# Another order of the seven products in the gate and up projections of a hybrid encoder block

## The chip, the cores and the metric

The kernel runs on one core of a Trainium2 chip. The metric is the device time of one execution in microseconds (us). TensorE multiplies; VectorE (DVE), ScalarE (ACT) and GpSimd (POOL) work on tiles, each taking the instructions of its own queue in order; SyncE (SP), ScalarE and GpSimd issue DMA transfers. GpSimd cannot reach the matmul banks (PSUM), so only VectorE and ScalarE read them.

## What is computed

One encoder block on x of 1024 rows by 1024 features, in float32:

```python
h = rmsnorm(x, norm1_g)
q, k, v, f_logit, u = split(h @ w_in)
attn = forgetting_attention(q, k, v, cumsum(log_sigmoid(f_logit + b_f)))   # 8 heads of 64
pool = multiscale_pool(u, w_pool, pool_scale)                              # windows 2, 4, 8, 16
x = x + concat(attn, pool) @ w_out
h2 = rmsnorm(x, norm2_g)
x = x + (silu(h2 @ w_gate) * (h2 @ w_up)) @ w_down                         # 1024 -> 2816 -> 1024
y = rmsnorm(x, final_g)
```

The change lies in the last product but one: `h2 @ w_gate` and `h2 @ w_up`, and the SwiGLU features made from them. The attention, the pooling, the first projections and the last norm are as they were.

## The kernel before

**Precision.** Every large product is done with operands split in two: ScalarE copies the source to a high part of reduced precision, VectorE subtracts it from the source for the low part (`split`, L119 to L121), and TensorE adds three matmuls, high x high, low x high and high x low (`mm3`, L159 to L163). A split weight operand of 128 x 1024 is called a page. Pages live in three slots that are used in turn (`gu_page`, L999), so the fourth page waits until TensorE is through with the first.

**Groups and products.** The 2816 features are worked in eleven groups (j = 0 to 10) of 256. In a group, the weights form a 2 x 2 block matrix (two halves of the features by two halves of the 1024 inputs), the normed rows another, and the four blocks of the result come from seven products P1 to P7 instead of eight (Strassen's scheme in Winograd's form). Four operands of the weight side are sums or differences, made by GpSimd in `gu_sums` (L1080): s1 = a21 + a22 for P5, s2 = s1 - a11 for P6, s3 = a11 - a21 for P7, s4 = a12 - s2 for P3; P1, P2 and P4 take a11, a12 and a22 as loaded. The raw halves (a11 and a12 in one buffer, a21 and a22 in the other) are loaded on SyncE's queue when the pages of the group before have been made (`gu_raw`, called in `next_page`, L1384 to L1388).

Each product is done for gate (n = 0) and up (n = 1), twelve matmuls of 512 columns each, into a pair of banks. P1, P6 and P5 add up in the same pair, c1, and after each of them ScalarE copies the pair out (`snap`, L1147, L1150): sP1 after P1, sU2 after P6, sU4 after P5. The next product of c1 must wait for the copy. P7 starts the pair c3 and P4 adds to it. `corner` (L1161) makes a feature block from c3 and a copy: h22 after P5 (c3 holds P7, with sU4), h21 after P3b (c3 holds P7 + P4, with sU2): VectorE adds the copy to gate (L1169) and up (L1171), ScalarE applies silu (L1170), GpSimd multiplies (L1172). h11 is sP1 + P2 and h12 is sU4 + P3. GpSimd then makes the sums f1 to f4 (L1176), and all blocks are stored by DMAs on ScalarE's queue (`spill`, L1272).

**Products in quarters.** In groups 1 to 10 P3, and in groups 3 to 10 (`BOTH = 3`) P2 as well, is split once more into seven quarter products Q1 to Q7 (`fine_product`, L1252), six matmuls of 256 columns each. VectorE adds each to the copy it belongs to (L1270). Three small banks hold them: Q1, Q6, Q5 and Q3 add up in bank A, Q7 and Q4 in bank B, Q2 is alone in C, and each of them has to wait until the add before it has read its bank. Their operands come in two pages, "a" (Q1, Q2, Q7, Q4) after one sum on VectorE and "b" (Q5, Q3, Q6) after three more (`fine_sums`, L1226 to L1231). The moving side needs small sums too, made once for P3 (b22) and once for P2 (b21) by the twelve `fine_steps` (L1187), spread over the product steps of groups 1 and 2.

**What sets the order.** A scheduler places the instructions of each engine by their readiness in its own timing model, with program order as priority; `tc.issue_after(ins)` puts what is traced in its block behind `ins` on the queue of the same engine. The main loop (L1393) goes through `todo`, with the products of groups 3 to 10 in the order `LAST`: P1, P6, P2a, P7, P2b, P5, P3a, P4, P3b. At each step it makes the page of the step after next, issues due stores, runs the product, and makes copies and features (`after`, L1279). `PIECES` (L1371) interleaves the quarters with a whole product: P2's with P7, P3's with P4. `mark` holds the last instruction of a kind: "page" and "hi" (last low and high part), "sum", "add" (last quarter add), "snap", "mm".

**Behind the groups** comes the output product with w_down, done in the same scheme over four sets of groups; its first pages and sums (`down_page`, L1358, `down_sum`, L1338) are made within group 10.

Of the kernel before, what the change touches and what calls it, by code (L numbers as in the profile page):

```python
# [45 lines left out]
def tile_kernel(  # L46
# [70 lines left out]
    mark = {}  # L117
# [956 lines left out]
    RING = 11  # L1074
# [5 lines left out]
    def gu_sums(j):  # L1080
        a11, a12, a21, a22 = gu_parts(j)
        s1, s2, s3, s4 = (xw_tile(f"s{i}", f"s{i}_{j}", (P, 2, 512)) for i in (1, 2, 3, 4))
        at = None
        for out, in0, in1, op in (
            (s1, a21, a22, ALU.add), (s2, s1, a11, ALU.subtract), (s3, a11, a21, ALU.subtract), (s4, a12, s2, ALU.subtract)
        ):
            with tc.issue_after(at.ins) if at and j >= BOTH else ExitStack():
                at = nc.gpsimd.tensor_tensor(out=out, in0=in0, in1=in1, op=op)  # L1088
        return dict(P1=a11, P2=a12, P6=s2, P7=s3, P5=s1, P3=s4, P4=a22)
# [57 lines left out]
    def snap(j, key, n):  # L1147
        tag = ("su", 2) if key == "sU2" else ("h", RING)
        t = snaps[j, key, n] = wk_tile(*tag, f"sn{j}_{key}{n}")
        mark["snap"] = nc.scalar.activation(out=t, in_=banks["c1", n], func=AF.Copy)  # L1150
# [101 lines left out]
    def fine_product(j, k, q, acc):  # L1252

        at = FINE_BANK[q]
        if q in ("Q1", "Q7", "Q2"):
            own = BANKS["c2", int(k == "P3")], 1
            fine_banks[at] = bank(f"fine{at}_{j}{k}", *(own if at == "C" else ("m", 2)))
        ps = fine_banks[at][:, QTR[0]]
        wh, wl = fine[j, k, q]
        bh, bl = fine[BLOCK[k], q]  # L1260
        for c in range(2):
            ws = slice(c * P, (c + 1) * P)
            mm3(
                ps, wh[:, ws], wl[:, ws], bh[:, c, :], bl[:, c, :],
                q in ("Q1", "Q7", "Q2") and c == 0, q in ("Q3", "Q4", "Q2") and c == 1, True,
            )
        n, h = FINE_TO[q]
        out = acc[n][:, QTR[h]]
        with tc.issue_after(mark["add"].ins) if q != "Q1" else ExitStack():
            mark["add"] = nc.vector.tensor_tensor(out=out, in0=ps, in1=out, op=ALU.add)  # L1270
# [97 lines left out]
    LAST = ("P1", "P6", "P2a", "P7", "P2b", "P5", "P3a", "P4", "P3b")  # L1368
# [5 lines left out]
    WINDOWS2 = {"P2a": (0, "P2", "P7"), "P7": (1, "P2", "P7"), "P2b": (2, "P2", "P7")}  # L1374
# [16 lines left out]

    waiting = []
    for i, (j, k) in enumerate(todo):  # L1393
        if i + 2 < len(todo) and k != "P2b":
            with ExitStack() as order:
                if k in ("P6", "P5") and j >= BOTH:
                    for ins in (mark["page"], mark["hi"]):
                        order.enter_context(tc.issue_after(ins.ins))
                    if k == "P5":
                        mark["P3a"] = mark["page"], mark["hi"]  # L1400
                        fine_sums(j, "P3", "b")
                        order.enter_context(tc.issue_after(mark["sum"].ins))
                next_page(*todo[i + 2])
        waiting.append(spills[:])
# [9 lines left out]
        elif k in window[j]:  # L1414
            step, little, whole = window[j][k]
            acc = [snaps[j, dict(P2="sP1", P3="sU4")[little], n] for n in range(2)]
            for piece in PIECES[step]:
# [8 lines left out]
        if k == "P2b":  # L1426
            with tc.issue_after(mark["add"].ins):
                next_page(*todo[i + 2])
        if (j, k) == (NG - 1, "P3b"):
            last_features = lambda j=j, k=k: after(j, k)  # L1430
        else:
            after(j, k)
        if j == NG - 1:
# [3 lines left out]
            if k == "P2a":  # L1437
                for key in ("P5", "P6"):
                    down_sum(0, key)
            if k == "P7":  # L1440
                for par in range(2):
                    down_load(par)
            if k == "P3a":
                with tc.issue_after(mark["add"].ins):
# [5 lines left out]
        if (j, k) == (BOTH - 1, "P1"):  # L1450
            q5, q7 = ([small(wk, f"g{n + m}", f"fine{n}{m}_b21") for m in range(2)] for n in (2, 4))
            finer += fine_steps("b21", q5, q7, ("g0", "g1"))
        for _ in range(min(3 if j == 1 and k in ("P1", "P2") else 2, len(finer))):
# [9 lines left out]
    with tc.issue_after(mark["add"].ins):  # L1463
        down_page(1)
# [178 lines left out]
```

## Time and profile before

| | |
|---|---|
| median of 3 runs | 1155.68 us (1153.98 to 1156.32) |
| profiled execution, its own time | 1151.23 us |
| its span, first to last instruction | 1149.4 us |
| mean granted clock of TensorE | 0.961 |
| TensorE busy, matmuls | 1054.1 us, 92% |
| VectorE busy | 797.8 us, 69% |
| ScalarE busy | 470.7 us, 41% |
| GpSimd busy | 412.8 us, 36% |

A profile is one execution, and times in it count from its first instruction. A row of the timeline has the start, the duration, the engine, the line of the kernel, the operation, the tile written and the tiles read, and in brackets how long the engine sat idle before it and what ended that. A row of the waits has the engine, tile and line that waited, what it waited for, and total, times and longest. Tile names leave numbers out: `gu_P` is a bank of the seven products, `gu_P_h` and `gu_P_l` the parts of a page, `r` the raw halves, `s` GpSimd's sums, `sn_sP` and `sn_sU` the copies, `b11`, `t2`, `t3`, `t1`, `t4` the moving blocks of P1, P6, P7, P5 and P4, `d` the output product.

### The profile page before, as it was taken

How to read it: one execution, taken by the hardware profiler on the slowest of the kernel's cores; microseconds unless marked ns; L12 is line 12 of the kernel's file. 1: busy time of each engine (PE TensorE's matmuls, PEld its weight loads, DVE VectorE, ACT ScalarE, POOL GpSimd, SP SyncE). 2: the span in 40 equal slices, each digit the busy share in tenths (PEclk: the TensorE clock that was granted, in tenths of full speed). 3: DMA queues.
4: the chain of work that ended last, by engine and by line, in shares of the span. 5: the costliest groups of instructions: out<-in, count | busy, mean ns of one | idle time of the engine just before them, and what ended most of it. 6: DMA issues, size and time to landing. Idle time of an engine off the chain costs nothing.

```text
span 1149.4 us, 15183 instructions
## 1 busy us (share of the span) xinstructions
PE 1054.1 (92%) x5428; PEld 895.5 (78%) x5428; DVE 797.8 (69%) x1224; ACT 470.7 (41%) x759; POOL 412.8 (36%) x316
## 2 busy tenths in 40 slices
PE   9999999999999979997977869797876899999997
PEld 8888889989888858886766757676765788888886
DVE  7365667668765958787566474655557589978787
ACT  7343556656643744342222232222223234333345
POOL 4430222133431507455355271726436340000035
PEclk9999999999999989999989889898989899999999
DMA  6225343237312513240321213131222576444423
GB/s 226 65 60 147 79 105 96 76 97 265 131 62 94 166 37 120 73 128 10 120 101 47 92 55 100 38 119 56 91 92 86 181 247 225 150 147 156 150 98 147
DMA packets 108859, 130.28 MB, mean 113 GB/s; under 512 B 8040, under 2 KB 71024, under 8 KB 108784
## 3 DMA queue, kind: packets, MB, share of 16 engines
q1 hardware_dynamic: 97216, 108.18, 30.0%
q10 hardware_dynamic: 10928, 19.42, 4.5%
q0 software_dynamic: 640, 1.71, 0.4%
q8 instruction: 43, 0.70, 0.2%
q14 instruction: 32, 0.26, 0.1%
HBM read 86.29 MB, written 33.03 MB: 104 GB/s over the span
## 4 chain that ended last, share of the span: by engine, by line
PE 33%; DVE 9%; POOL 4%; ACT 3%; DMA 3%; issue 2%; SPq 1%; POOLq 0%; ACTq 0%; DVEq 0%
PE d L162 5%; PE d L163 5%; PE d L161 5%; PE gu_P L161 5%; PE gu_P L162 4%; PE gu_P L163 4%; POOL s L1088 3%; DVE gu_P_l L121 2%; DMA r<-in_w_up_dram 2%; DVE s L1231 1%; ACT gu_P_h L120 1%; DVE gu_P3a_l L121 1%; DVE r L1231 1%; DVE sn_sU L1303 1%; SPq L1048 1%
## 5 line engine op out<-in xcount | busy, mean ns | idle before, releaser
L162 PE MATMUL d<-d,d 128*128 128x512 f32 (+1 forms) x308 | 119.2, 389 | 0.5 <-DVE d L121 0.5
L163 PE MATMUL d<-d,d 128*128 128x512 f32 (+1 forms) x308 | 119.0, 388 | 0.0
L629 POOL TENSOR_SCALAR p<-p,rr 128x128 f32<-128x128 f32 (+3 forms) x64 | 48.7, 768 | 176.0 <-DVE rr L628 131.8
L161 PE MATMUL d<-d,d 128*128 128x512 f32 x308 | 107.8, 388 | 0.0
L121 DVE TENSOR_TENSOR gu_P_l<-s,gu_P_h 128x1024 fp32r<-128x1024 f32 (+1 forms) x38 | 62.1, 1644 | 41.2 <-ACT gu_P_h L120 41.2
L161 PE MATMUL gu_P<-t2h,gu_P_h 128*128 128x512 f32 x88 | 43.2, 491 | 50.3 <-ACT sn_sP L1150 50.3
L120 ACT ACTIVATE d<-r_f 128x1536 fp32r<-128x1536 f32 (+1 forms) x28 | 38.7, 1384 | 114.1 <-PE d L162 111.6
L120 ACT ACTIVATE gu_P_h<-s 128x1024 fp32r<-128x1024 f32 (+1 forms) x38 | 36.3, 964 | 97.2 <-POOL s L1088 39.1
L162 PEld LDWEIGHTS d<-d,d 128*128 128x128 f32 x308 | 57.8, 188 | 13.0 <-DVE d L121 1.1
L161 PEld LDWEIGHTS d<-d,d 128*128 128x128 f32 x308 | 57.8, 188 | 11.9
L163 PEld LDWEIGHTS d<-d,d 128*128 128x128 f32 x308 | 57.8, 188 | 11.8
L161 PEld LDWEIGHTS gu_P<-t2h,gu_P_h 128*128 128x128 f32 x88 | 21.1, 240 | 58.5 <-ACT sn_sP L1150 53.7
L1296 POOL TENSOR_TENSOR sn_sP<-sn_sP,sn_sP 128x512 f32<-128x512 f32 x8 | 14.9, 1863 | 137.6 <-ACT sn_sP L1295 137.6
L1172 POOL TENSOR_TENSOR h<-h,qh 128x512 f32<-128x512 f32 x25 | 43.4, 1737 | 57.1 <-ACT qh L1170 51.6
L1494 POOL TENSOR_SCALAR sse<-sse 128x1 f32<-128x1 f32 x7 | 3.5, 496 | 167.0 <-ACT junk L1490 167.0
L626 ACT ACTIVATE p<-p,mn 128x128 f32<-128x128 f32 (+3 forms) x64 | 49.3, 772 | 31.7 <-DVE mn L620 28.8
L648 DVE TENSOR_TENSOR tl<-tp,th 128x512 fp32r<-128x512 f32 (+1 forms) x80 | 49.5, 633 | 9.7 <-ACT th L647 8.7
L121 DVE TENSOR_TENSOR gu_P_l<-r,gu_P_h 128x1024 fp32r<-128x1024 f32 x24 | 48.3, 2012 | 6.6 <-ACT gu_P_h L120 6.6
L121 DVE TENSOR_TENSOR d<-r_f,d 128x1536 fp32r<-128x1536 f32 (+1 forms) x28 | 47.5, 1695 | 6.7 <-ACT d L120 6.7
L163 PE MATMUL qk<-hTh,l_qk 128*128 128x512 f32 x128 | 50.7, 396 | 0.0
L161 PE MATMUL qk<-hTh,h_qk 128*128 128x512 f32 x128 | 50.6, 395 | 0.0
L162 PE MATMUL qk<-hTl,h_qk 128*128 128x512 f32 x128 | 50.4, 394 | 0.0
(1174 smaller groups left out, 3462.4 us busy)
## 6 DMA issues: line engine op xcount, KB each, us to landing
r_f<-hsdP SPq DMA_DIRECT2D x77, 256.0 KB
r<-in_w_gate_dram SPq DMA_DIRECT2D x44, 256.0 KB
r<-in_w_up_dram SPq DMA_DIRECT2D x44, 256.0 KB
r_wd<-in_w_down_dram SPq DMA_DIRECT2D x22, 512.0 KB
hsdP<-f ACTq DMA_DIRECT2D x40, 256.0 KB
s<-hi SPq DMA_DIRECT2D x64, 128.0 KB
hsdP<-h ACTq DMA_DIRECT2D x23, 256.0 KB
x<-in_x_dram SPq DMA_DIRECT2D x8, 512.0 KB
```

The source lines that it names most:

```text
L120: mark["hi"] = nc.scalar.activation(out=hi, in_=src, func=AF.Copy)
L121: return eng.tensor_tensor(out=lo, in0=src, in1=f32(hi), op=ALU.subtract)
L161: nc.tensor.matmul(ps, lh, rh, start=start, stop=False, **kw)
L162: nc.tensor.matmul(ps, lh, rl, start=False, stop=False, **kw)
L163: mark["mm"] = nc.tensor.matmul(ps, ll, rh, start=False, stop=stop, **kw)
L626: nc.scalar.activation(out=pr[:, :n], in_=pr[:, :n], func=AF.Exp, scale=-1.0, bias=mn, accum_out=rs)
L629: nc.gpsimd.tensor_scalar(out=pr[:, :n], in0=pr[:, :n], scalar1=rr, scalar2=1.0, op0=ALU.mult, op1=ALU.mult)
L648: nc.vector.tensor_tensor(out=tl[:, :w], in0=tp[:, :w], in1=f32(th[:, :w]), op=ALU.subtract)
L1088: at = nc.gpsimd.tensor_tensor(out=out, in0=in0, in1=in1, op=op)
L1172: nc.gpsimd.tensor_tensor(out=h, in0=h, in1=q, op=ALU.mult)
L1231: mark["sum"] = nc.vector.tensor_tensor(out=out, in0=in0, in1=in1, op=op)
L1296: nc.gpsimd.tensor_tensor(out=acc[1], in0=acc[1], in1=acc[0], op=ALU.mult)
```

## The change

In groups 3 to 10 the order becomes P1, P7, P2a, P6, P2b, P5, P3a, P4, P3b, and P2's quarters go among P6 (`PIECES2`), with Q4 ahead of the second half of the first bank's product and Q6 behind it; P3's quarters among P4 take the same pattern. GpSimd makes s3 before s1, s2 and s4. P2a's page is made behind the copies of P1 on ScalarE. P3's first sum goes behind P5's low part on VectorE, and P3a's page behind that; the last quarter add of P2 goes behind P3a's low part; P7's low part goes behind the add of Q5. The copies of P1 in groups 0 and 1 get buffers of their own. The fine steps of b21 start a step earlier and at another pace (`PACE`), so that they end with P7 of group 2. The first two sums of the output product move behind its second page.

```diff
@@ -1081,9 +1081,12 @@
         a11, a12, a21, a22 = gu_parts(j)
         s1, s2, s3, s4 = (xw_tile(f"s{i}", f"s{i}_{j}", (P, 2, 512)) for i in (1, 2, 3, 4))
         at = None
-        for out, in0, in1, op in (
+        todo = [
             (s1, a21, a22, ALU.add), (s2, s1, a11, ALU.subtract), (s3, a11, a21, ALU.subtract), (s4, a12, s2, ALU.subtract)
-        ):
+        ]
+        if j >= BOTH:
+            todo.insert(0, todo.pop(2))
+        for out, in0, in1, op in todo:
             with tc.issue_after(at.ins) if at and j >= BOTH else ExitStack():
                 at = nc.gpsimd.tensor_tensor(out=out, in0=in0, in1=in1, op=op)
         return dict(P1=a11, P2=a12, P6=s2, P7=s3, P5=s1, P3=s4, P4=a22)
@@ -1145,7 +1148,7 @@
     snaps = {}
 
     def snap(j, key, n):
-        tag = ("su", 2) if key == "sU2" else ("h", RING)
+        tag = ("su", 2) if key == "sU2" else (f"g{n}", 1) if key == "sP1" and j < 2 else ("h", RING)
         t = snaps[j, key, n] = wk_tile(*tag, f"sn{j}_{key}{n}")
         mark["snap"] = nc.scalar.activation(out=t, in_=banks["c1", n], func=AF.Copy)
 
@@ -1266,7 +1269,11 @@
             )
         n, h = FINE_TO[q]
         out = acc[n][:, QTR[h]]
-        with tc.issue_after(mark["add"].ins) if q != "Q1" else ExitStack():
+        with ExitStack() as order:
+            if q != "Q1":
+                order.enter_context(tc.issue_after(mark["add"].ins))
+            if (k, q) == ("P2", "Q3"):
+                order.enter_context(tc.issue_after(mark["page"].ins))
             mark["add"] = nc.vector.tensor_tensor(out=out, in0=ps, in1=out, op=ALU.add)
 
     def spill(due, q=nc.scalar):
@@ -1365,13 +1372,16 @@
         return lows
 
     LATER = ("P1", "P2", "P6", "P7", "P5", "P3a", "P4", "P3b")
-    LAST = ("P1", "P6", "P2a", "P7", "P2b", "P5", "P3a", "P4", "P3b")
+    LAST = ("P1", "P7", "P2a", "P6", "P2b", "P5", "P3a", "P4", "P3b")
     todo = [(j, k) for j in range(NG) for k in (LAST if j >= BOTH else LATER if j else FIRST)]
     finer = []
     PIECES = (
         ("Q1", "Q2", "Q7", (0, (0, 1)), (0, (2, 3)), "Q6", "Q4"), ((1, (0, 1)), "Q5", (1, (2, 3))), ("Q3",),
     )
-    WINDOWS2 = {"P2a": (0, "P2", "P7"), "P7": (1, "P2", "P7"), "P2b": (2, "P2", "P7")}
+    PIECES2 = (
+        ("Q1", "Q2", "Q7", (0, (0, 1)), "Q4", (0, (2, 3)), "Q6"), ((1, (0, 1)), (1, (2, 3)), "Q5"), ("Q3",),
+    )
+    WINDOWS2 = {"P2a": (0, "P2", "P6"), "P6": (1, "P2", "P6"), "P2b": (2, "P2", "P6")}
     WINDOWS3 = {"P3a": (0, "P3", "P4"), "P4": (1, "P3", "P4"), "P3b": (2, "P3", "P4")}
     window = {j: dict(WINDOWS3 if j else {}, **(WINDOWS2 if j >= BOTH else {})) for j in range(NG)}
 
@@ -1389,18 +1399,24 @@
             if k == ("P3b" if j else "P4"):
                 operands[j + 1] = gu_sums(j + 1)
 
+    PACE = {(1, "P1"): 3, (1, "P2"): 3, (2, "P1"): 2, (2, "P2"): 2, (2, "P6"): 3, (2, "P7"): 3}
     waiting = []
     for i, (j, k) in enumerate(todo):
-        if i + 2 < len(todo) and k != "P2b":
+        if i + 2 < len(todo) and (j < BOTH or k != "P1"):
             with ExitStack() as order:
-                if k in ("P6", "P5") and j >= BOTH:
-                    for ins in (mark["page"], mark["hi"]):
-                        order.enter_context(tc.issue_after(ins.ins))
+                if j >= BOTH and k == "P3b":
+                    order.enter_context(tc.issue_after(mark["add"].ins))
+                if j >= BOTH and k in ("P7", "P6", "P2b", "P5"):
                     if k == "P5":
-                        mark["P3a"] = mark["page"], mark["hi"]
                         fine_sums(j, "P3", "b")
-                        order.enter_context(tc.issue_after(mark["sum"].ins))
+                    for name in ("page", "hi") + (("sum",) if k in ("P2b", "P5") else ()):
+                        order.enter_context(tc.issue_after(mark[name].ins))
                 next_page(*todo[i + 2])
+            if j >= BOTH and k == "P6":
+                with tc.issue_after(mark["page"].ins):
+                    fine_sums(j, "P3", "a")
+            if k == "P2b":
+                mark["P3a"] = mark["page"], mark["hi"]
         waiting.append(spills[:])
         spills.clear()
         while len(waiting) > (1 if j < BOTH else 3):
@@ -1414,7 +1430,7 @@
         elif k in window[j]:
             step, little, whole = window[j][k]
             acc = [snaps[j, dict(P2="sP1", P3="sU4")[little], n] for n in range(2)]
-            for piece in PIECES[step]:
+            for piece in (PIECES2 if j >= BOTH else PIECES)[step]:
                 with tc.issue_after(mark["mm"].ins):
                     if isinstance(piece, str):
                         fine_product(j, little, piece, acc)
@@ -1423,34 +1439,31 @@
         elif i:
             for n in range(2):
                 product(j, k, n)
-        if k == "P2b":
-            with tc.issue_after(mark["add"].ins):
-                next_page(*todo[i + 2])
         if (j, k) == (NG - 1, "P3b"):
             last_features = lambda j=j, k=k: after(j, k)
         else:
             after(j, k)
+        if j >= BOTH and k == "P1":
+            with tc.issue_after(mark["snap"].ins):
+                next_page(*todo[i + 2])
         if j == NG - 1:
             if k == "P1":
                 for par in range(2):
                     down_raw(0, par)
-            if k == "P2a":
-                for key in ("P5", "P6"):
-                    down_sum(0, key)
-            if k == "P7":
+            if k == "P6":
                 for par in range(2):
                     down_load(par)
             if k == "P3a":
-                with tc.issue_after(mark["add"].ins):
+                with tc.issue_after(mark["add"].ins), tc.issue_after(mark["hi"].ins):
                     down_page(0)
         if (j, k) == (0, "P4"):
             t = const.tile([P, 2, 2, 256], R, tag="wmask", bufs=1, name="fine1_b22")
             q7 = small(wk, "e2", "fine3h_b22"), small(xw, "junk2", "fine3l_b22")
             finer += fine_steps("b22", (t[:, 0, :, :], t[:, 1, :, :]), q7, ("e0", "e1"))
-        if (j, k) == (BOTH - 1, "P1"):
+        if (j, k) == (BOTH - 2, "P3b"):
             q5, q7 = ([small(wk, f"g{n + m}", f"fine{n}{m}_b21") for m in range(2)] for n in (2, 4))
             finer += fine_steps("b21", q5, q7, ("g0", "g1"))
-        for _ in range(min(3 if j == 1 and k in ("P1", "P2") else 2, len(finer))):
+        for _ in range(min(PACE.get((j, k), 2 if j < 2 else 0), len(finer))):
             with tc.issue_after((mark["page"] if j else mark["h22", 0]).ins):
                 finer.pop(0)()
         pages.pop((j, k))
@@ -1461,7 +1474,10 @@
     nc.sync.dma_start(out=gfb, in_=final_g.partition_broadcast(P))
     closing = mark["mm"]
     with tc.issue_after(mark["add"].ins):
-        down_page(1)
+        lows = down_page(1)
+    with tc.issue_after(lows[1].ins):
+        for key in ("P5", "P6"):
+            down_sum(0, key)
     with tc.issue_after(mark["hi"].ins):
         last_features()
     for k in ("P7", "P4"):
```

## The prediction, made before the changed kernel was run

> **What bounds the kernel now.** I read the page first, then the waits of TensorE, then TensorE's timeline through the groups of the gate and up products, then ScalarE and VectorE ahead of the longest wait, and last the chain of waits there.
>
> ```profile
> span 1149.4 us, 15183 instructions
> ...
> PEclk9999999999999989999989889898989899999999
> ```
>
> ```profile
> PE gu_P L161 <- ACT sn_sP L1150: 50.3, 8, 7.6
> PE gu_P L161 <- DVE qh L1169: 12.7, 8, 1.8
> ...
> PE fineA_2P L161 <- DVE sn_sU L1270: 2.9, 1, 2.9
> ```
>
> The first two rows of the waits (us in total, times, longest) happen eight times each: once in each of the groups 3 to 10, which split both P2 and P3. The longer one is P6's first matmul waiting for the copies of P1's banks (L1150). The granted clock dips in just that stretch of the page's row. TensorE's timeline (start, duration) shows one such wait, and unit prices:
>
> ```profile
> 528.51 0.39 PE L161 MATMUL gu_P<-b11h,gu_P_h 128*128 128x512 f32 x1
> ...
> 643.56 0.28 PE L161 MATMUL fineA_5P<-b21h,gu_P2a_h 128*128 128x256 f32 x1
> ...
> 645.71 0.40 PE L161 MATMUL gu_P<-t3h,gu_P_h 128*128 128x512 f32 x1
> ...
> 648.46 0.28 PE L161 MATMUL fineA_5P<-fine2h_b,gu_P2b_h 128*128 128x256 f32 x1
> ...
> 679.21 0.39 PE L163 MATMUL gu_P<-b11h,gu_P_l 128*128 128x512 f32 x1
> 686.45 0.80 PE L161 MATMUL gu_P<-t2h,gu_P_h 128*128 128x512 f32 x1 [6.86 <-ACT sn_sP L1150]
> ...
> 691.74 0.49 PE L161 MATMUL gu_P<-t2h,gu_P_h 128*128 128x512 f32 x1
> ...
> 932.17 0.40 PE L161 MATMUL d<-d,d 128*128 128x512 f32 x1
> ```
>
> Group 3's P1 starts at 528.51 and the output product at 932.17: eight groups in 403.7 us, 50.5 each. Three quarter products take 645.71 - 643.56 = 2.15, so one takes 0.72; half a product (12 matmuls) takes 648.46 - 645.71 = 2.75, a whole one 5.5. A group holds five whole products and fourteen quarters: 5 x 5.5 + 14 x 0.72 = **37.5 us** of matmuls without a wait. The other 13 us are idle: 6.86 at P6, and behind it 12 matmuls in 691.74 - 686.45 = 5.29 instead of 2.75, half speed, 2.5 more; 1.8 at P4; the rest at P3's first piece and in small gaps. So these eight groups are bound by a loop through the other engines, not by TensorE.
>
> ScalarE and VectorE just ahead of that wait:
>
> ```profile
> 683.91 1.06 ACT L120 ACTIVATE gu_P2a_h<-r 128x1024 fp32r<-128x1024 f32 x1 [2.59 <-DVE r L1231]
> 684.88 1.04 ACT L120 ACTIVATE gu_P_h<-s 128x1024 fp32r<-128x1024 f32 x1
> 685.82 1.06 ACT L1150 ACTIVATE sn_sP<-gu_P 128x512 f32<-128x512 f32 x2
> ```
>
> ```profile
> 679.59 0.41 DVE L1270 TENSOR_TENSOR sn_sU<-fineA_5P,sn_sU 128x256 f32<-128x256 f32 x1
> 679.92 0.67 DVE L1169 TENSOR_TENSOR qh<-gu_P,sn_sU 128x512 f32<-128x512 f32 x1
> ...
> 685.00 1.23 DVE L121 TENSOR_TENSOR gu_P2a_l<-r,gu_P2a_h 128x1024 fp32r<-128x1024 f32 x1 [1.17 <-ACT gu_P2a_h L120]
> 686.14 2.30 DVE L121 TENSOR_TENSOR gu_P_l<-s,gu_P_h 128x1024 fp32r<-128x1024 f32 x1
> 688.36 3.25 DVE L1231 TENSOR_TENSOR r<-r 128x256 f32<-128x256 f32 x3
> ...
> 695.90 0.95 DVE L121 TENSOR_TENSOR gu_P2b_l<-r,gu_P2b_h 128x768 fp32r<-128x768 f32 x1
> ```
>
> P1 is over at 679.4, so its banks could be copied then. But the copies stand on ScalarE behind the high part of P2a, which waits for P2's first sum on VectorE, and behind P7's high part. The wait belongs to the order of ScalarE's queue, not to the data.
>
> **The change, part by part.** Times in this part count from P1's first matmul. P1 and the floating Q3 of the group before end at 5.5 + 0.7 = 6.2.
>
> *P7 runs second.* P7 opens banks of its own (c3), so no copy of P1 stands before it; P6, which does need the copies, comes 5.5 + 2.15 later, at 13.9. That takes out 6.86 and the slow clock's 2.5. P7 has new conditions. Its page needs GpSimd's a11 - a21, now the first sum, not the third:
>
> ```profile
> 663.25 1.23 DVE gu_P_l L121
> ...
> 670.48 2.38 POOL s L1088
> ```
>
> From P4's low part (the last reader of the raw half that these loads refill) to the first sum takes 670.48 - 664.48 = 6.0, the sum 2.4, P7's high part 1.04, its low part at the longer price 2.30: 11.7 us. P4 cannot start before that same low part, and after it PE has P4 with three quarters (5.5 + 2.2) and P1 with Q3 (6.2), 13.9. Cover 2.2 us: cost nothing. If it went, P7 would wait for the excess.
>
> P7 also starts c3 anew, so h21's reads of c3 (L1169, then L1171) must be over; before, P6 and P2a lay between. qh ended at 680.59, 1.2 after P1's end. It follows Q3's add, which stood behind a low part made of the second GpSimd sum; now that low part is P7's, from the first. Bounds 0 and 1.2; I take 0.2, nearer to nothing because the source is there a whole sum earlier. P7's low part in turn is now held behind Q5's add, which is due when P1 starts; behind it on VectorE stand Q3's add and h21, so a late P7 page would delay these reads, and P7 waits for both alike.
>
> *Copies ahead of P2a's high part.* Copies 6.2 to 7.3 (1.06), high part to 8.3, low part to 9.6 (1.23). P2a is due at 11.7: hidden with 2.1 to spare.
>
> *P2's pieces among P6, and Q4 early.* In the new order Q4 follows six matmuls (1.4) behind Q7, and accumulates in Q7's bank, so it needs Q7's add to have read it. It is due at 11.7 + 2.15 + 1.4 = 15.2. VectorE's queue after P2a's low part: P6's low part (2.30) to 11.9, P2's three later sums (3.25) to 15.1, three adds of 0.41 to 16.4. So Q4 waits about 1.2. If P2b's high part (three quarters of 1.06, so 0.8 by estimate) and low part (0.95) go before Q7's add too, as P2b's low part does now, it waits 2.9. I take 1.7, nearer to the first since P2b's page cannot start until P7 has freed its slot. The same quarter order in P3: h22's reads and P3b's low part stand before the adds; 0 to 0.3, taken 0.1.
>
> *U2's copies between P6 and P5.* P6 and P5 share c1; between them only Q5 and Q3 (1.4 us) are left. Each copy takes 0.53, the first half is complete 2.75 earlier, and P5's second half is needed 2.75 later: nothing. Behind the copies on ScalarE stands P3a's high part; P3a is a whole product away.
>
> *P3's first sum behind P5's low part.* It no longer waits for P2's last add, so P3a's page, P3's later sums and P4's low part come earlier against PE, and h22's reads too: the 1.8 at P4 and the wait at P3a go. P2's last add now stands behind P3a's low part; only the activation of h11 and the release of a bank wait for that, neither due before P3a.
>
> *Spills.* The five stores of the previous group's h21 and f1 to f4 stay behind P5's high part on ScalarE's queue, but P5's high part comes about 11 us sooner, against the end of f4 on GpSimd. If f4 is late, U2's copies wait behind the stores; no row shows that. Bounds 0 and 1, taken 0.
>
> Per group: 0.2 + 1.7 + 0.1, and 0.3 for small gaps, is 2.3 us of waits: **39.8 us**.
>
> *Fine steps of b21 earlier.* In group 2 they delay the adds that Q4 and Q5 of P3 wait for:
>
> ```profile
> 519.48 2.20 DVE L1207 TENSOR_TENSOR fine_b<-fine_b,fine_b 128x512 f32<-128x512 f32 x1
> ```
>
> Now they are done by P7 of group 2. The 2.9 us wait goes; ends 0 (the steps hinder another product) and 2.9, taken 2.9, since nothing in P1 to P7 of group 2 reads quarter banks.
>
> *Down sums later.* Two sums leave idle VectorE time in group 10 for the busy stretch behind the second down page:
>
> ```profile
> 899.31 1.23 DVE L1342 TENSOR_TENSOR sumP<-r_wd 128x1024 f32<-128x1024 f32 x1 [3.44 <-PE gu_P L163]
> ```
>
> Two at 1.23 are 2.5 us; hidden fully or not at all. I take 2.5, as the adds and low parts of the next step stand right behind them. The buffers g0 and g1 for early copies, and the third order edge on the first down page, cost nothing: off every chain above.
>
> **Sum.** 403.7 - (8 x 39.8 + 0.7 for the Q3 that overhangs) = 84.6 off; 2.9 off; 2.5 on: 85.0 off. The profiled execution took 1151.2 us (span 1149.4 and 1.8 around it): 1066.2. The median of the three runs, 1155.7, is 4.5 above it: **1071 us**.
>
> **Rivals.**
>
> *VectorE and GpSimd stand in each other's way.* P7's low part, of the same size as P2a's of 1.23 us, took 2.30 when it began at 686.14, inside the second of these; and that one, of the size of the first, had begun just after P2a's low part at 685.00:
>
> ```profile
> 683.51 1.44 POOL L1176 TENSOR_TENSOR f<-sn_sU,h 128x512 f32<-128x512 f32 x1
> 685.03 2.33 POOL L1176 TENSOR_TENSOR f<-f,sn_sP 128x512 f32<-128x512 f32 x1
> ```
>
> ```profile
> 686.45:737.45 51.00, 41.42 (x205) 34.33 (x205) 30.32 (x37) 14.30 (x20) 24.06 (x12) 0.90 0.24 78
> ```
>
> The window's fifth and seventh entries, VectorE 30.3 and GpSimd 24.1 us, had 51 us to avoid each other; now they have 39. If the two never overlapped and VectorE never found PSUM work meanwhile: VectorE at least 7 x 1.23 + 2 x 0.95 of low parts, 8 sums at 0.4, as an add of that width, and h12 at twice that (4.0), 14 adds and 4 reads (14 x 0.41 + 4 x 0.67 = 8.4); GpSimd 4 sums of 2.4 and 7 shorter pieces at 1.44 (19.7). Together 42.6 us a group: 8 x 2.8 = 22 us more than forecast, 1093. For it: both engines' work moves into P1, P7 and P2a. Against: the adds and reads of PSUM do overlap now. The Trainium skill (SBUF — State Buffer, Who interferes with whom) says that a VectorE instruction with two SBUF inputs and a GpSimd one that reads SBUF hold one read interface in turn, the later one blocked to the end. By that rule the rival is the ceiling of this effect, and it speaks against the change; the rows agree (2.30 is the rest of GpSimd's 2.33 and then 1.1).
>
> *The copies stay behind P2a's high part* (the edge does not do what it says). P7 still need not wait. P2a's high part would come as late as now, 683.91 or 10.7 after P1's start, with its low part done at 13.0, so P2a waits 1.3: 10 us on top, 1081.
>
> *c3 takes the copies' place.* If h21's reads queue on VectorE behind P2a's low part, or that and P6's: 6.2 + 1.06 + 1.06 + 1.23 (+ 2.30) + 0.41 + 0.67 = 10.6 or 12.9; P7 waits 4.4 or 6.7 and pays 2.5 for the clock: 44.7 to 47.0 a group with the 0.3 of small gaps, 1110 to 1128. Against: the reads come from earlier steps and need only Q3's add.
>
> *Slower:* the same reads behind P2's three sums too, with both low parts at 2.30: 6.2 + 2.1 + 4.6 + 3.25 + 0.41 + 0.67 = 17.2, P7 waits 11.0, 13.5 with the clock, 51.3 a group: 7 us more than before with the other two terms, 1163. It decides from 13.0 us of waits a group, which is where 50.5 is reached.
>
> **How the numbers follow.** The forecast (waits of 0.8 to 3.5 a group, 1059 to 1080) has 0.55; the VectorE and GpSimd rival 0.22; the copies staying behind 0.05; c3 0.13; slower 0.04; something near no change 0.01. With all covers holding, 38.1 a group, it is 1057; with 1.2 at P7, 2.9 at Q4 and 1.8 still at P4, 43.4 a group, 1100. The range is 1056 to 1102: forecast and the next two rivals, 0.82. A measurement here can tell about 0.2%, 2.3 us, from no change. Faster by more: 0.94; within: 0.02; slower: 0.04.
>
> **What would show it.** Right: TensorE's waits have no row for P1's copies (L1150) any more, P1 to P1 takes 38 to 41 us, the granted clock stays near 1 in the groups, and the largest new wait is the A or B quarter bank on VectorE's add. Wrong: a wait of P7 on L1169 or L1171 above 1.2 us a group, P5 waiting for U2's copies, VectorE busy over 95% of a group, or a group above 43.4 us.

## The result and the profile after

The kernel after takes 1078.9 us (median of 4 runs, 1077.3 to 1080.4), the kernel before 1154.8 in the same comparison: a ratio of 0.935, with an interval of 0.932 to 0.938. The forecast was 1071.0, with a range of 1056 to 1102. The profiled execution took 1080.4 us. Two lines of its page:

```profile
span 1078.6 us, 15149 instructions
...
PEclk9999999999999999999999999999999989999999
```

The dips of the granted clock through the groups are gone; one is left near the end. The waits of TensorE (releaser; us in total, times, longest):

```profile
PE gu_P L161 <- ACT sn_sU L1308: 11.0, 7, 1.7
PE d L162 <- DVE d L121: 4.0, 1, 4.0
PE fineA_2P L161 <- DVE sn_sU L1277: 2.7, 1, 2.7
PE gu_P L161 <- ACT sn_sU L1153: 2.5, 3, 1.1
PE gu_P L163 <- DVE gu_P_l L121: 2.2, 1, 2.2
PE fineB_4P L161 <- DVE sn_sP L1277: 1.5, 1, 1.5
```

P6's 50.3 us for P1's copies (L1150 before, L1153 now) and P4's 12.7 us for h22's reads are not there any more. New are P7's first matmul in seven groups (first row), the output product (second), and Q4 behind Q7's add in each group (last row, one of its kind). The points of TensorE's timeline (start, duration) that divide the run:

```profile
520.52 0.63 PE L161 MATMUL gu_P<-b11h,gu_P_h 128*128 128x512 f32 x1
...
652.07 0.47 PE L161 MATMUL gu_P<-t3h,gu_P_h 128*128 128x512 f32 x1 [1.58 <-ACT sn_sU L1308]
...
662.77 0.39 PE L161 MATMUL fineB_6P<-b21h,gu_P2a_h 128*128 128x256 f32 x1 [1.44 <-DVE sn_sP L1277]
...
693.08 0.47 PE L161 MATMUL gu_P<-t3h,gu_P_h 128*128 128x512 f32 x1 [1.47 <-ACT sn_sU L1308]
...
853.02 0.40 PE L161 MATMUL d<-d,d 128*128 128x512 f32 x1
...
871.64 0.79 PE L162 MATMUL d<-d,d 128*128 128x512 f32 x1 [4.03 <-DVE d L121]
```

P7 to P7 is 693.08 - 652.07 = 41.0 us. The three stretches (up to group 3's P1; groups 3 to 10; from the output product to the end of the span) were 528.5, 403.7 and 217.2 us before; they are now 520.5, 853.02 - 520.52 = 332.5 (41.6 a group), and 1078.6 - 853.02 = 225.6. So the profiled span lost 8.0 and 71.2, and got 8.4 back: 70.8 us.

### The profile page after: what moved, and what is told of

It is laid out like the page before. It is cut to its first block, busy times and chain, and to the rows that moved or that the text cites. A ratio compares the mean times of both kernels' runs of the same rounds, so it can differ in the third digit from the quotient of the medians.

```text
span 1078.6 us, 15149 instructions
## 1 busy us (share of the span) xinstructions
PE 1032.6 (96%) x5428; PEld 881.0 (82%) x5428; DVE 766.0 (71%) x1224; ACT 470.0 (44%) x759; POOL 403.4 (37%) x316
## 5 line engine op out<-in xcount | busy, mean ns | idle before, releaser
L162 PE MATMUL d<-d,d 128*128 128x512 f32 (+1 forms) x308 | 120.9, 393 | 4.0 <-DVE d L121 4.0
L163 PE MATMUL d<-d,d 128*128 128x512 f32 (+1 forms) x308 | 120.2, 392 | 0.0
L161 PEld LDWEIGHTS d<-d,d 128*128 128x128 f32 x308 | 58.1, 189 | 14.2 <-ACT d L120 1.7
L1175 POOL TENSOR_TENSOR h<-h,qh 128x512 f32<-128x512 f32 x25 | 47.5, 1899 | 45.0 <-ACT qh L1173 39.2
L121 DVE TENSOR_TENSOR gu_P_l<-s,gu_P_h 128x1024 fp32r<-128x1024 f32 (+1 forms) x38 | 53.9, 1428 | 6.7 <-ACT gu_P_h L120 6.6
L1614 DVE TENSOR_TENSOR x2f_s<-d,x2f_s 128x512 f32<-128x512 f32 x64 | 42.8, 685 | 13.6 <-PE d L163 13.6
L647 ACT ACTIVATE th<-tp 128x512 fp32r<-128x512 f32 (+1 forms) x80 | 42.4, 550 | 15.6 <-PE tp L643 12.7
L1153 ACT ACTIVATE sn_sU<-gu_P 128x512 f32<-128x512 f32 x44 | 26.0, 590 | 50.6 <-PE gu_P L163 25.0
L1303 POOL TENSOR_TENSOR sn_sP<-sn_sP,sn_sP 128x512 f32<-128x512 f32 x8 | 11.4, 1421 | 96.8 <-ACT sn_sP L1302 96.8
```

The lines of the kernel that those rows point to most:

```text
L121: return eng.tensor_tensor(out=lo, in0=src, in1=f32(hi), op=ALU.subtract)
L161: nc.tensor.matmul(ps, lh, rh, start=start, stop=False, **kw)
L162: nc.tensor.matmul(ps, lh, rl, start=False, stop=False, **kw)
L163: mark["mm"] = nc.tensor.matmul(ps, ll, rh, start=False, stop=stop, **kw)
L647: nc.scalar.activation(out=th[:, :w], in_=tp[:, :w], func=AF.Copy)
L1175: nc.gpsimd.tensor_tensor(out=h, in0=h, in1=q, op=ALU.mult)
```

## The experiments

Each run's ratio is to the kernel before, measured beside it; one per cent is 11.5 us. The stretches are those just named, from each run's own trace.

| Run | Edit | Median us | Ratio (95% interval) | To group 3 | Groups | End |
|---|---|---|---|---|---|---|
| before | | 1154.8 | 1 | 528.5 | 403.7 | 217.2 |
| after | | 1078.9 | 0.935 (0.932 to 0.938) | 520.5 | 332.5 | 225.6 |
| e1 | before + early buffers | 1144.2 | 0.993 (0.990 to 0.995) | 519.5 | 405.4 | 217.2 |
| e2 | before + copies first | 1115.1 | 0.967 (0.965 to 0.969) | 530.6 | 366.4 | 217.2 |
| e5 | after, copies behind | 1079.5 | 0.935 (0.933 to 0.938) | 520.6 | 332.8 | 224.5 |
| e9 | after, P3's sum behind P2 | 1131.5 | 0.981 (0.979 to 0.983) | 519.9 | 384.4 | 225.6 |
| e10 | e5 and e9 together | 1133.6 | 0.982 (0.980 to 0.984) | 520.9 | 386.1 | 225.1 |
| e7 | after, old fine steps | 1081.3 | 0.937 (0.935 to 0.940) | 523.6 | 332.1 | 224.3 |
| e3 | after, sums at P2a | 1074.7 | 0.932 (0.930 to 0.934) | 521.2 | 336.1 | 216.4 |
| e8 | after, sums behind page 0 | 1071.2 | 0.929 (0.926 to 0.931) | 520.7 | 333.6 | 217.9 |
| e4 | after, Q3 early | 1064.7 | 0.924 (0.922 to 0.926) | 521.6 | 319.8 | 225.0 |
| e6 | after, Q4 later | 1082.7 | 0.938 (0.936 to 0.941) | 520.6 | 335.8 | 224.5 |
| c1 | e4 and e8 together | 1059.4 | 0.919 (0.917 to 0.921) | 520.0 | 319.7 | 217.9 |
| c2 | c1 and Q4 later | 1059.0 | 0.918 (0.916 to 0.920) | 522.3 | 317.6 | 217.8 |

**e1: the early buffers alone.**

```diff
-        tag = ("su", 2) if key == "sU2" else ("h", RING)
+        tag = ("su", 2) if key == "sU2" else (f"g{n}", 1) if key == "sP1" and j < 2 else ("h", RING)
```

> The kernel before, with one part of the change alone: group 0's and group 1's copies of P1 go to buffers of their own (g0, g1) instead of the ring h. Theory: the change's first stretch became shorter by 8.0 us (group 3's P1 at 528.51 before, at 520.52 after) because these copies no longer wait for a free buffer of the ring, so that the wait of 8.59 us at 417.32 goes. Expected here: that wait under 1 us, copies of group 0 near 402 and 405 instead of 417.7, and the whole 6 to 9 us faster than before (ratio 0.992 to 0.995). Rival, the prediction's term: the buffers are off every chain, 0 us, and the 8 us come from the fine steps of b21 and from the new order of the products; then the wait of 8.59 stays and the ratio is 0.999 to 1.001.

The time fell by 8.6 us (before took 1152.7 beside it), all of it ahead of group 3. In the kernel before, TensorE and ScalarE in group 0:

```profile
417.32 0.79 PE L161 MATMUL gu_P<-t3h,gu_P_h 128*128 128x512 f32 x1 [8.59 <-ACT gu_P_h L120]
...
424.77 0.39 PE L161 MATMUL gu_P<-t2h,gu_P_h 128*128 128x512 f32 x1
```

```profile
417.72 1.06 ACT L1150 ACTIVATE sn_sP<-gu_P 128x512 f32<-128x512 f32 x2
```

and in this experiment:

```profile
408.72 0.39 PE L161 MATMUL gu_P<-t2h,gu_P_h 128*128 128x512 f32 x1
...
419.60 0.39 PE L161 MATMUL gu_P<-t3h,gu_P_h 128*128 128x512 f32 x1
```

```profile
399.65 0.58 ACT L1150 ACTIVATE sn_sP<-gu_P 128x512 f32<-128x512 f32 x1
```

The wait was P7 (t3) for its own page, as the row says; but P7 stood in front only because P6 (t2) could not run without the copies. With the copies 18 us earlier, P6 fills the time in which P7's page is made. The row of the wait does not name the copies at all.

**e2: the copies ahead of P2a's high part, in the old order of products.**

```diff
-        if i + 2 < len(todo) and k != "P2b":
+        if i + 2 < len(todo) and k != "P2b" and (j < BOTH or k != "P1"):
...
+        if j >= BOTH and k == "P1":
+            with tc.issue_after(mark["snap"].ins):
+                next_page(*todo[i + 2])
```

> The kernel before, with one part of the change alone: in the groups 3 to 10 the page of P2a is made behind the copies of P1's banks, so that the copies stand ahead of P2a's high part on ScalarE; the order of the products stays P1, P6. Theory A: most of the 50.5 us of a group came from the place of the copies in ScalarE's queue. P6 follows P1 directly, so it still waits about 0.8 for the last copy (1.06 for two, the first can start under P1's second half), P2a's high part is 1.1 later than it was, and nothing else becomes late: 6.86 + 2.5 - 0.8 = 8.5 less a group, 42.0 a group, 68 us less, near 1087 (ratio 0.935 to 0.950); the order of the products is then worth little. Theory B (the loop through VectorE and GpSimd holds P2a and P7 at their places anyway, and only P7 in second place gives it cover): the wait moves from P6 to P2a or P7 and half or less of it goes, ratio 0.96 to 0.99.

The time lies in theory B's range: 45.8 us a group, about half of the change's gain in the groups. Theory B's reason does not hold, though: no wait moved to P2a or P7, and the new one at P2b is 0.5 to 1.1 us in five groups. TensorE's waits:

```profile
PE gu_P L161 <- ACT sn_sP L1150: 14.9, 8, 3.1
PE gu_P L161 <- DVE qh L1169: 12.7, 8, 1.8
```

P6's wait fell from 50.3 to 14.9, 1.9 a group where 0.8 was expected; P4's stayed at 12.7. Behind P4's 1.8 us, half of a product (12 matmuls) took 4.4 us for 2.75 in three of seven groups, and 2.9 in the other four, as in all seven of before.

**e5, e9 and e10: parts undone.** e5 makes P2a's page at the top of P1's step, ahead of the copies:

```diff
-        if i + 2 < len(todo) and (j < BOTH or k != "P1"):
+        if i + 2 < len(todo):
...
-        if j >= BOTH and k == "P1":
-            with tc.issue_after(mark["snap"].ins):
-                next_page(*todo[i + 2])
```

e9 gives back the old place of P3's first sum:

```diff
-            if (k, q) == ("P2", "Q3"):
-                order.enter_context(tc.issue_after(mark["page"].ins))
...
-                with tc.issue_after(mark["page"].ins):
-                    fine_sums(j, "P3", "a")
...
+        if k == "P2b":
+            with tc.issue_after(mark["add"].ins):
+                next_page(*todo[i + 2])
+            mark["P3a"] = mark["page"], mark["hi"]
```

e10 does both, so that in the groups only the new order of products is left.

> The kernel after, with the page of P2a made at the top of P1's step again, so that P2a's high part stands ahead of the copies of P1's banks on ScalarE (the place that it has in the kernel before); P7 stays second. The prediction priced this as a rival: P2a's high part comes as late as before and P2a waits 1.3 us a group, 10 us on top of after's 1078.9, near 1089 (ratio 0.943). Theory now, with the copies-only kernel at 45.8 us a group: the two edits overlap, since with P7 second the copies have a product of 5.5 us to hide behind; the price is at most the prediction's, 0 to 10 us (ratio 0.935 to 0.944). Rival: P7's own high part stands behind the copies and the late P2a page, P7 waits for it, and the group goes back to 45 us or more: ratio 0.96 or above.

> The kernel after, with P3's first sum and P3a's page where the kernel before has them: behind P2's last add on VectorE, not behind P5's low part. P7 second, the copies ahead and the rest stay. The prediction's term: P4's wait of 1.8 us and P3a's wait (0.8 and more) come back in each of the eight groups, so 8 x 1.8 to 8 x 3 = 14 to 24 us on top of after, near 1093 to 1103 (ratio 0.947 to 0.956). Rival: the early P7 already gives P3a's page its lead, since P2's last add now falls due 5 us sooner against P4; then the place of the sum is worth under 3 us (ratio 0.933 to 0.938).

> The kernel after with two of its edits undone in the groups 3 to 10: the copies of P1's banks stand behind P2a's high part again, and P3's first sum behind P2's last add. What is left there is the new order of the products, with P2's pieces among P6. Theory: with P7 second the place of the copies is worth nothing (undone alone: 1079.5 for 1078.9), and the place of P3's sum is worth 52 us (undone alone: 1131.5), so both undone are 1131 plus or minus 4 (ratio 0.978 to 0.985). Rival: the late copies push P2's adds (they add into these copies), P2's last add and with it the sum behind it come later still, and the two add up to more than each alone: 1140 to 1150 (ratio 0.988 to 0.997), so that the new order alone is worth next to nothing.

e5 takes as long as after: with P7 second, the place of the copies is worth nothing in sum. The copies do come late there, for P6 in six groups:

```profile
661.56 0.50 PE L161 MATMUL gu_P<-t2h,gu_P_h 128*128 128x512 f32 x1 [1.24 <-ACT sn_sP L1153]
```

In the same groups Q4, which follows six matmuls later, does not wait any more (1.4 in after): one wait took the place of the other. e9 costs 52 us, two to four times what was expected from the old waits, and more than half of the change's gain. Its VectorE and TensorE:

```profile
644.62 0.42 DVE L1275 TENSOR_TENSOR sn_sP<-fineA_5P,sn_sP 128x256 f32<-128x256 f32 x1 [5.30 <-PE fineA_5P L163]
644.96 0.41 DVE L1234 TENSOR_TENSOR s<-s 128x256 f32<-128x256 f32 x1
646.56 1.23 DVE L121 TENSOR_TENSOR gu_P3a_l<-s,gu_P3a_h 128x1024 fp32r<-128x1024 f32 x1 [1.18 <-ACT gu_P3a_h L120]
```

```profile
646.58 0.39 PE L161 MATMUL fineA_5P<-b22h,gu_P3a_h 128*128 128x256 f32 x1 [1.53 <-ACT gu_P3a_h L120]
...
647.84 0.39 PE L163 MATMUL fineA_5P<-b22h,gu_P3a_l 128*128 128x256 f32 x1 [0.76 <-DVE gu_P3a_l L121]
...
651.80 0.80 PE L161 MATMUL gu_P<-t4h,gu_P_h 128*128 128x512 f32 x1 [1.22 <-DVE qh L1172]
```

P3's sum waits for P2's last add, and that for TensorE (5.30); the sum begins only 1.6 us ahead of P3a's first matmul, and the page has to be made in between. TensorE stands 1.53 + 0.76 + 1.22 = 3.5 us, and the rest of the 6.5 us a group is mostly half-speed matmuls behind these waits. In after the same sum ran at 665.96 and P3a began at 675.36, without a wait. e10 is as e9: the losses do not add up, and the order of products, without P3's early sum, shortens the groups by 18 us of 71. The wait for P1's copies is down to 10.0 us there, but P7 waits 1.2 us in each of seven groups, and P3a 2.3 instead of 0.9.

So the early sum is needed, and with it the new order suffices. Whether the old order would do as well with the copies ahead and an early sum for P3 was not run. The copies alone already gave 37 us in the old order (e2: 366.4 us of groups), more than the new order with the copies ahead but without the early sum (e9: 384.4). What the new order itself is worth stays open.

**e7: the fine steps of b21 at their old place and pace.**

```diff
-        if (j, k) == (BOTH - 2, "P3b"):
+        if (j, k) == (BOTH - 1, "P1"):
...
-        for _ in range(min(PACE.get((j, k), 2 if j < 2 else 0), len(finer))):
+        for _ in range(min(3 if j == 1 and k in ("P1", "P2") else 2, len(finer))):
```

> The kernel after, with the fine steps of b21 at their old place and pace (behind group 2's P1, two at a time). The prediction gave the earlier place 2.9 us; the wait that it named is still there in after, 2.7 for 2.9, and a wait of 2.2 us of P7 of group 2 for its low part is new. Theory: the earlier steps bring nothing, and the kernel with the old place takes as long as after, within 2 us (ratio 0.932 to 0.938). Rival, the prediction's term: 2.9 us slower. Third: the earlier steps cost the 2.2 us at P7 that are new, and the old place is 1 to 3 us faster.

The median is 2.4 us above after's, the intervals overlap: not settled by the time. The wait of 2.7 (group 2, bank A) is here 3.0 (bank B), so the earlier steps did not take it away; bank B's wait in group 2 was 1.6 in before and is 0.4 in after. To group 3, e7 is 3.1 us longer, of which 1.6 is a slow clock behind P7's wait that comes in some runs and not in others (last section). P7's 2.2 is 2.1 here, and 1.8 in e1: it comes with the early buffers, not with the steps.

**e3 and e8: the two down sums.** Both take them from behind the second page. e3 has them back at group 10's P2a:

```diff
+            if k == "P2a":
+                for key in ("P5", "P6"):
+                    down_sum(0, key)
...
```

e8 has them right behind the first down page:

```diff
                 with tc.issue_after(mark["add"].ins), tc.issue_after(mark["hi"].ins):
-                    down_page(0)
+                    lows = down_page(0)
+                with tc.issue_after(lows[1].ins):
+                    for key in ("P5", "P6"):
+                        down_sum(0, key)
...
```

> The kernel after, with the down sums of P5 and P6 back at group 10's P2a, where the kernel before has them. Theory: the tail became 8.4 us longer (from 932.17 to 1149.4 before, from 853.02 to 1078.6 after) because the two sums stand ahead of the second down page's adds and low parts: the wait of 4.0 us of d on the low part goes, and with it the slow clock behind it. Expected: 5 to 8 us faster than after (near 1072, ratio to before 0.928 to 0.931), the tail near 218 us. Rival 1, the prediction's size: 2.5 us faster (near 1076). Rival 2: the sums push group 10's own low parts instead, or the tail is longer because the output product's first inputs come late whatever the sums do: no change within 2 us.

> The kernel after, with the down sums of P5 and P6 directly behind the low parts of the first down page, where VectorE has idle stretches of 1.07, 1.68, 0.77 and 1.07 us between 846 and 853, instead of behind the second page. With the sums back at group 10's P2a the tail was 9.2 us shorter (216.4 for 225.6) and group 10 was 4.5 us longer, as the sums stood ahead of P3a's and P4's low parts. Theory: it is only a matter of what stands behind the two sums on VectorE; here only two adds of quarter banks and the second page's low part do, so the tail is near 217 and group 10 at most 1 us longer: 7 to 9 us less, near 1071 (ratio 0.926 to 0.930). Rival: the sums push the second page's low parts and the tail's first products wait for these: no better than the sums at P2a (ratio 0.931 or above).

In both, the end is as short as before (216.4 and 217.9 us). e3 pays 3.6 us for it in the groups, e8 1.1, so e8 is the better place. VectorE in after, with the sums (L1349) behind the second page:

```profile
857.03 2.31 DVE L1349 TENSOR_TENSOR sumP<-r_wd 128x1024 f32<-128x1024 f32 x1
...
861.66 1.33 DVE L1349 TENSOR_TENSOR sumP<-r_wd,sumP 128x1024 f32<-128x1024 f32 x1
...
866.97 4.62 DVE L121 TENSOR_TENSOR d<-sumP,d 128x1024 fp32r<-128x1024 f32 x1
```

```profile
866.91 2.36 POOL L1349 TENSOR_TENSOR sumP<-r_wd,sumP 128x1024 f32<-128x1024 f32 x1
869.22 1.27 POOL L1179 TENSOR_TENSOR f<-h,f 128x512 f32<-128x512 f32 x1
```

The sums took 2.31 and 1.33 us, and pushed the low part that TensorE needs next into GpSimd's own sum and the last of its feature sums: 4.62 us for one that takes 1.2 elsewhere. TensorE waited 4.03 (the row at 871.64 above). The windows of the two kernels, after first, then e8 (last three columns: granted clock, DMA share, GB/s):

```profile
865.00:880.00 15.00, 10.19 (x30) 7.22 (x29) 12.13 (x12) 2.01 (x3) 7.03 (x7) 0.77 0.62 216
```

```profile
866.00:881.00 15.00, 13.89 (x62) 11.28 (x61) 15.00 (x19) 5.21 (x6) 5.85 (x7) 1.00 0.74 268
```

Clock 0.77 and 30 recorded matmuls, against 1.00 and 62.

**e4: P3's last quarter Q3 ahead of the second half of the next P1.**

```diff
-                product(j, k, n)
+                with tc.issue_after(q3.ins) if n and k == "P1" and j > BOTH else ExitStack():
+                    product(j, k, n)
+        if k == "P3b":
+            q3 = mark["mm"]
```

> The kernel after, with P3's last quarter Q3 ahead of the second half of the next group's P1 on TensorE (it stood behind all of P1, directly ahead of P7). Theory: P7's wait of 1.5 us in each of seven groups (11.0 us in all) is the chain Q3's end, Q3's add on VectorE, h21's read of the bank that P7 opens anew. With Q3 some 2.7 us earlier the chain is hidden: 7 x 1.5 = 10.5 us less, at most 8 x 1.7 = 13.6, if nothing takes its place; near 1068 (ratio 0.922 to 0.927), no wait of P7 above 0.3. Rival 1: the wait is for the silu of h12 (L1308), as the row names it, or for P7's own page; then it stays and the time is that of after. Rival 2: Q3 now comes before its own inputs (P3b's low part) or before Q5's add, and PE waits there for as long as it did at P7: within 2 us of after.

12.7 us less in the groups, 39.6 us from P7 to P7, and no row for P7 in the waits. So the 11 us were the chain behind Q3. VectorE in after:

```profile
650.57 0.43 DVE L1234 TENSOR_TENSOR r<-r 128x256 f32<-128x256 f32 x1 [2.29 <-POOL s L1091]
650.91 0.42 DVE L1277 TENSOR_TENSOR sn_sU<-fineA_5P,sn_sU 128x256 f32<-128x256 f32 x1
651.24 0.68 DVE L1172 TENSOR_TENSOR qh<-gu_P,sn_sU 128x512 f32<-128x512 f32 x1
```

Q3's matmuls stood behind all of P1 and ended at 650.5; Q3's add followed P2's first sum, which had waited 2.29 us for GpSimd; then came h21's read of the bank that P7 opens, to 651.92, and P7 began at 652.07. The row names the silu of h12 (L1308), which ended at 651.99, 0.07 behind the read, but P7 uses no tile of that silu; e5's row for the same wait names the read (L1172).

**e6: Q4 six matmuls later**, and **c1 and c2: the edits together.**

```diff
-        ("Q1", "Q2", "Q7", (0, (0, 1)), "Q4", (0, (2, 3)), "Q6"), ((1, (0, 1)), (1, (2, 3)), "Q5"), ("Q3",),
+        ("Q1", "Q2", "Q7", (0, (0, 1)), (0, (2, 3)), "Q4", "Q6"), ((1, (0, 1)), (1, (2, 3)), "Q5"), ("Q3",),
```

> The kernel after, with Q4 behind the whole first half of the bank product in both windows (P2's among P6, P3's among P4) instead of in its middle, six matmuls later. Theory: Q4's wait of 1.4 us a group for Q7's add in P2's window is only a matter of distance: 1.37 us of matmuls more cover it, 8 x 1.4 = 11 us less, near 1068 (ratio 0.923 to 0.928), if nothing takes its place. Rival: P2's adds then come later on VectorE too (Q4's own add stands ahead of P5's low part), the wait moves to the next product (P2b's or P5's low part) and to Q3's float, and half or less of it is won: ratio 0.929 to 0.935.

> The kernel after with two of the single edits together: Q3 ahead of P1's second half, and the down sums of P5 and P6 behind the first down page. The first took 14.2 us off after's median, the second 7.6, by their ratios 1.05 and 0.6 per cent of before. They touch different stretches (the groups 3 to 10, and the output product), so theory: they add up, ratio 0.918 to 0.921, near 1059. Rival: with the groups 1.6 us shorter the loads of the output product's first features come late, and half of one gain is lost: ratio 0.922 or above.

> The same two edits, and Q4 behind the whole first half of the bank product. On after alone Q4's later place was 3.5 us slower, although Q4's wait went: P7's wait grew from 1.5 to 2.5 us a group, as everything on VectorE up to Q3's add came later, and 24 matmuls of P7 took 7.1 us for 5.5 behind the longer waits. Theory: with Q3 ahead of P1's second half that chain has 2.75 us of matmuls to hide behind, so the later Q4 now wins its 1.4 us a group: 8 to 11 us below the kernel without it, near 1049 (ratio 0.908 to 0.912). Rival: VectorE is the bound of the group by then (its busy share in a steady group is near 90 per cent), and the 1.4 us turn up at other waits: within 3 us of the kernel without it.

In e6 Q4's wait goes in all groups but one, and P7's grows to 17.3 us in seven groups: the groups are 3.3 us longer, not 11 shorter. c1 is the sum of its parts, as expected. c2 gains nothing that can be told from c1 by the medians: its groups are 2.1 us shorter, but the stretch ahead of them, in which the edit changes no order, came out 2.3 longer. And the rival reason in its expectation is wrong: VectorE is not near its limit. A group of c1 (TensorE, weight loads, VectorE, ScalarE, GpSimd busy), and one of c2:

```profile
678.00:717.60 39.60, 38.08 (x206) 32.31 (x205) 26.08 (x36) 14.57 (x20) 22.36 (x12) 1.00 0.31 100
```

```profile
679.20:718.50 39.30, 38.18 (x205) 32.46 (x204) 28.51 (x36) 14.31 (x19) 23.69 (x12) 1.00 0.31 101
```

VectorE is busy 66% of c1's group. In c2 the same 36 instructions take 2.4 us longer. One of them, beside GpSimd's sum:

```profile
685.12 2.36 DVE L1310 TENSOR_TENSOR sn_sU<-sn_sU,sn_sU 128x512 f32<-128x512 f32 x1
```

```profile
684.53 2.41 POOL L1091 TENSOR_TENSOR s<-r,s 128x1024 f32<-128x1024 f32 x1
```

It took 0.68 in c1, where it began after GpSimd's sums; here it is over 0.5 us after GpSimd's ends at 686.94. The Trainium skill (SBUF — State Buffer, Who interferes with whom) has the later of two such instructions blocked to the end of the other; these two rows agree. P2's first sum stands behind it, and with that P2a's page, so Q7's add comes late against Q4 again (0.7 to 1.2 us of wait in seven of the groups). P2's first sum starts 1.1 us later behind P1 than in c1: about 0.5 is this instruction, the rest is that GpSimd's sums, which it needs as well, end later.

c1 and c2 are the fastest kernels of the study, about 20 us under after; c1, with one edit less, takes 1059.4 us, 0.919 of before.

## Why the prediction was right, and where its sizes were off

The loop through VectorE and ScalarE opened, as forecast: the row for P1's copies is gone, and TensorE is busy for 38 of 41 us in a group (entries of the window: TensorE, weight loads, VectorE, ScalarE, GpSimd, clock, DMA share, GB/s):

```profile
643.42:684.54 41.12, 38.10 (x205) 32.46 (x204) 25.24 (x36) 14.23 (x19) 22.68 (x12) 1.00 0.30 97
```

The sum was 85.0 us; the profiled executions differ by 70.8. That the total still fell into the forecast's own 1059 to 1080 is in part luck. A group has 41.6 - 37.5 = 4.1 us beside its matmuls, where that range stood for 0.8 to 3.5; the 8 us ahead of group 3, mostly from buffers that were priced at nothing, made up for it.

The prediction gave 9.4 us of the 10.7 a group to the order ("6.86 and the slow clock's 2.5", for P7 in second place). The runs do not bear that out: without P3's early sum the order gains 2.2 us a group (e10), and in the old order the copies' edge alone gains 4.7 (e2).

- **P7's start was mis-sized**, at 0.2 us a group with bounds of 0 and 1.2; it was 1.6 in seven groups (11.0 in all), above the upper bound. The step "the source is there a whole sum earlier" looked at the low part alone. What counted was Q3's place on TensorE, directly ahead of P7 (e4), and P2's first sum, which stands ahead of Q3's add. The prediction had named a wait of P7 above 1.2 as a sign of being wrong, and 38 to 41 us from P1 to P1 as a sign of being right. Only two of the eight groups lie within these bounds (39.2 and 41.0; the others 41.1 to 44.2), but the mean of 41.6 is under the limit of 43.4.
- **Q4's wait** was taken at 1.7 and was 1.4 to 1.5 in seven groups, 1.1 in group 3. P5's wait for U2's copies, taken as nothing and named as a sign of being wrong, was 1.4 us in two of the eight groups together (the third in its row lies in group 2). With the 37.5 us of matmuls, 1.58 at P7 and 1.44 at Q4, 0.6 is left of the 41.1 from group 5's P1 to group 6's.
- **P3's first sum** got half a sentence ("the 1.8 at P4 and the wait at P3a go"). That was right, but not its weight: in the new order 52 us hang on it (e9). Of the rows of before, 12.7 us at P4 and 0.8 a group at P3a did not show that price. There the chain was 0.9 us late at P3a, in e9's shorter group 2.3, and behind P4's wait the matmuls ran at full speed in before (12 in 2.9 us) and at half speed in e9 (6 in 2.7).
- **The copies' edge** is worth 37 us in the old order (e2) and nothing in the new (e5). The rival priced its failure at 1.3 us a group, at P2a. P2a waited for nothing in e5; 1.24 came at P6, and Q4's wait went in its place.
- **The early buffers** were taken as "off every chain" and were worth 8 to 9 us (e1). The rows were read as P7 waiting for its page; why P7 stood ahead of P6 was not asked.
- **The fine steps** were to take away 2.9 us; 2.7 of that wait is still there, and what they gain elsewhere is not settled (e7).
- **The down sums** were sized at 2.5, their own length, and cost 8.4: the low part behind them ran into GpSimd's work, and the wait slowed TensorE's clock (e8).
- **The rival of VectorE and GpSimd** gave 42.6 us a group as a floor without overlap; after is at 41.6 and c1 at 39.6, so it does not bind. VectorE was busy 30.3 us in a group of before (51.0 us) and 25.2 in one of after (41.1): after the change fewer of them collide. Its mechanism is real, though: it sets the end of after and takes part of c2's gain.

Of the 14.2 us between 85.0 and 70.8, 13.4 lie in the groups, and 9.4 of these at P7 (11.0 less eight times 0.2); the end adds 5.9, and the early buffers give 5.1 back.

## What to carry to other kernels

Before an edit is costed at nothing, ask what order the wait has forced: a row names the page that came last, not the copy that kept another product from filling the time. Price a wait with the half-speed matmuls that may come behind it, and an added vector instruction with what the one queued behind it will then run beside. When a product is moved, look up what TensorE runs directly ahead of its new place, as the whole chain behind that now lies bare.

## What the runs showed of the hardware

The clock of TensorE falls after some waits of about 2 us, and not after others of the same length. In e6 P7 waited 2.11 us and then ran its first matmuls 0.43 us apart:

```profile
653.72 0.76 PE L161 MATMUL gu_P<-t3h,gu_P_h 128*128 128x512 f32 x1 [2.11 <-ACT sn_sU L1308]
...
654.71 0.63 PE L163 MATMUL gu_P<-t3h,gu_P_l 128*128 128x512 f32 x1
655.14 0.63 PE L161 MATMUL gu_P<-t3h,gu_P_h 128*128 128x512 f32 x1
```

Its 24 took 7.1 us for the 5.5 of a product; in after, behind 1.58 us, they took 5.56. In e6 itself P7 waited 2.14 us in group 7, and its 24 matmuls took 5.53. At group 2's P7, the 20 matmuls behind a wait of 2.18 took 4.66 us in after, and those behind one of 2.05 took 6.26 in e7. In e2 even the half product behind P6's wait of 3.10 us took 2.89. The Trainium skill (TensorE: Matmul & The Clock Gate, What's actually happening) puts the fall after an idle window of about 3.4 us; here it came after 2.05 and 2.11 us, and the measurement decides.
